# Small TensorE products moved behind the next projection at each phase opening, and the sigmoid table loaded earlier

## The chip, the cores and the metric

The kernel runs on one core of one Trainium2 chip. Its time is the device time in microseconds (us) of one execution; three runs of the kernel before lie between 1514.94 and 1518.55 us, with a median of 1517.14 us. Five engines work side by side, each through its own instructions in order: TensorE (PE, with its weight loads shown apart as PEld), VectorE (DVE), ScalarE (ACT), GpSimd (POOL) and SyncE (SP, which starts the transfers).

## The reference

Two layers work on 256 positions of width 1024, in float32. Each layer has three sub-layers, and each sub-layer is wrapped in two norms.

```
x = x + 0.5 * rmsnorm(swiglu(rmsnorm(x, g)))      # FFN 1
h = rmsnorm(x, g);  P = h @ W_in                  # mixer: one projection,
A, B, C = ssd(P), retention(P), attention(P)      #   columns split among three branches
y = sum_m sigmoid(gate_m) * (branch_m @ W_branch_m)
x = x + rmsnorm(y @ W_out)
x = x + 0.5 * rmsnorm(swiglu(rmsnorm(x, g)))      # FFN 2
```

swiglu is (silu(a) * b) @ W_out, where a and b are the two halves of x @ W_in. The attention has 16 query heads and 2 key/value heads and a window of 128 positions.

## The kernel before

The 256 positions are two tiles of 128 rows, t = 0 and t = 1. Every large product is made of three fast float32 products: a value is split into a rounded part and a remainder (`split`, L66: ACT rounds, DVE subtracts), and `mm3` (L86) adds up high by low, high by high and low by high. These are the rows L88 and L89 on PE. A projection of one tile t by 512 columns (`gemm`, L96) takes 8 steps of K, 24 matmuls, and adds up in one PSUM buffer `acc`. The weights come by DMA into `raw` and are split into `hl` by `units` (L71).

A phase is one sub-layer, and there are six: FFN 1, mixer, FFN 2, twice. Five times one phase ends while the next opens, and that is the place of this change:

- The phase that ends runs `close` (L308). Its last projection leaves a PSUM buffer, from which `posthalf` (L192) takes a sum of squares (ACT, L196) and a product with the gain (`yg`, DVE, L197). `postnorm` (L200) makes the factor `r` on POOL (`rstd`, L138: an add at L141, a power at L143) and updates `x` of tile 1 on DVE, in two halves (L206).
- The phase that opens needs `x` transposed. `prenorm` (L169) does it with 8 PE transposes for each tile (L178), which ACT and DVE copy out as `xT` (L182, L185), and it takes the sum of squares (L150) from which POOL makes the factor `pr`. Tile 0 is made inside the last projection of the old phase. Tile 1 is made inside an early projection of the new phase: `gemm` calls `do()` at step `at`, and two `after` edges (L105 to L110) fix its 8 transposes between two steps of that projection.
- In an FFN the opening's order is chunk 0 then chunk 1 of tile 0; the transposes of tile 1 stand in chunk 1, at step 2 (L327). Between the two chunks the first result is ready for use: `swiglu` (L121) makes `sl` by a Silu on ACT (L125) and `h` on DVE (L127), and `transposed` (L153) turns `h` by two PE transposes (L161) into `hT`.
- In the mixer `kvdt(0)` (L756) makes keys, values and the step sizes of tile 0 in one projection of 272 columns, and `main("aq0", 0, ...)` (L789) the first queries, with the transposes of tile 1 at step 5. Between them `att_kv` (L357) splits the keys (`kh` on ACT L367, `kl` on DVE L368), takes the values (`vn`, L371), and turns both by small PE products (L375, L379). `att_q` (L382) does the same for queries (L394).

What the program writes is not the order in which the engines get it. A scheduler that follows a simulated time line orders the instructions of each engine, within the data's dependencies and the edges that the program adds: `add_manual_dep` (in `after`, L91) and `issue_after(ins)`. The latter adds an edge to `ins` from each instruction of its block that runs on the engine of `ins`, and leaves the other engines free.

ACT holds the function tables of one set at a time; the row ACT_TABLE_LOAD shows where another set is brought in. The mixer uses Exp and Tanh, the FFN uses Silu. There are five such loads: at the start (L871), at the Exp of `mixer_consts` (L730, twice) and at the first Silu of each FFN 2 (L125, twice).

Of the kernel before, what the change touches and what calls it, by code (L numbers as in the profile page):

```python
# [10 lines left out]
AF = mybir.ActivationFunctionType  # L11
# [29 lines left out]
class Trunk:  # L41
# [54 lines left out]
    def gemm(self, xT, t, slots, width=512, at=None, do=None):  # L96

        ps = self.acc.tile([P, 512], F32, tag="acc", name="acc")
        n = len(slots)
        ts = slice(t * P, t * P + P)  # L100
        mid = []
        for k, (wh, wl) in enumerate(slots):
            x = xT[k // 2]
            if do and k == at:
                mid = do()  # L105
                for i in mid:
                    self.after(i, m[2])
            m = self.mm3(ps[:, :width], x[:, k % 2, 0, ts], x[:, k % 2, 1, ts], wh, wl, k == 0, k == n - 1)
            for i in mid:
                self.after(m[0], i)  # L110
            mid = []
        return ps

    def gemmT(self, ps, xT, slots, c0):
# [193 lines left out]
    def close(self, order, gemm, at, gpost, scale, nxt):  # L308

        yg, ss = {}, [self.small(2, "ss") for t in range(NT)]
        for n, t in order:
            last = (n, t) == (1, 1) and nxt
            ps = gemm(n, t, at if last else None, (lambda: nxt(0)) if last else None)
            yg[t, n] = self.posthalf(n, ps, gpost, scale, ss[t])
            if n:
                self.postnorm(t, [yg[t, 0], yg[t, 1]], ss[t], 4 * EPS, nxt is None)
        self.second = (lambda: nxt(1)) if nxt else None

    def ffn(self, i, l, xT, nxt):
        nc, A = self.nc, self.A
        xT, r = xT
        w = A[f"w_ffn{i}_in"][l]
        hT, slots = [], {}
        order = [(0, 0), (1, 0), (0, 1), (1, 1)] + [(c, t) for c in range(2, NFC) for t in range(NT)]
        at, where = 2, (1, 0)  # L327
        if self.first:
            order[1:3] = [(0, 1), (1, 0)]
            at, where = 5, (0, 0)  # L330
        for c, t in order:
            if c not in slots:
                with self.tc.issue_after(self.opened.ins) if self.first and not c else ExitStack():
                    slots[c] = self.units(w, 2 * c, fine=c < 2) + self.units(w, 2 * c + 1, fine=c < 2)
                hT += self.new_T(1, "hT")
            ps = self.gemm(xT, t, slots[c], 512, at, self.second if (c, t) == where else None)
            h = self.swiglu(ps[:, 0:256], ps[:, 256:512], r[t])
            self.transposed(hT[c:c + 1], h, t)
            if (c, t) == (2, 1) and self.first:
                self.first = None  # L340
                self.tables()
        gpost = self.gain(f"ffn{i}_post_g", l)
        slots = self.ffn_out_slots(i, l)
        nxT, nx = nxt() if nxt else (None, None)
        self.close([(0, 0), (0, 1), (1, 0), (1, 1)],
                   lambda n, t, at, do: self.gemm(hT, t, slots[n * KF:n * KF + KF], 512, at, do),
                   KF - 4, gpost, 2.0, nx)
        return nxT
# [386 lines left out]
    def mix(self, l, xT, nxt):  # L735
        nc, A = self.nc, self.A
# [19 lines left out]
        def kvdt(t):  # L756
            ps = self.gemm(xT, t, skv, 272)
            nc.vector.scalar_tensor_tensor(out=dtx[:, t], in0=ps[:, 256:272], scalar=r[t], in1=self.dtb,
                                           op0=ALU.mult, op1=ALU.add)
            self.att_kv(t, ps)  # L760

        def main(key, t, slots, at=None, do=None):
            ps = self.gemm(xT, t, slots, 512, at, do)
            n = int(key[2]) if len(key) > 2 else 0
            if key[:2] == "aq":
                self.att_q(n, t, ps)
            elif key[:2] == "rv":
                if n == 0:
                    S[f"rv{t}"] = self.t4([D], name="rv")
                o = S[f"rv{t}"][:, 512 * n:512 * n + 512]  # L770
                if n:
                    nc.scalar.activation(out=o, in_=ps, func=AF.Copy, scale=r[t])
                else:
                    nc.vector.tensor_scalar(out=o, in0=ps, scalar1=r[t], scalar2=None, op0=ALU.mult)
                S[f"rv{n}{t}"] = True
            elif key[:2] == "rg":
                g = self.silu2(ps, rh[t])
                nc.vector.scalar_tensor_tensor(out=g, in0=g, scalar=r[t], in1=gret[:, 512 * n:512 * n + 512],
                                               op0=ALU.mult, op1=ALU.mult)
                S[f"rg{n}{t}"] = g  # L780
            elif key[0] == "z":
                S[f"z{key[1]}{t}"] = self.silu2(ps, rh[t])
            else:
                self.rotate(key, t, ps)
            self.pump()

        kvdt(0)
        s0 = W(0)
        main("aq0", 0, s0, 5, self.second)  # L789
        scales(1)  # L790
        kvdt(1)
        S["dt"] = dtx
        pr = self.pbank()
        for t in range(NT):
            nc.tensor.transpose(pr[:, t], r[t].to_broadcast([P, P]), self.ident)
        S["rT"] = self.sm.tile([P, T], F32, tag="rT", bufs=1, name="rT")
        self.copy(S["rT"], pr[:, 0:2].rearrange("p t n -> p (t n)"))
        main("aq0", 1, s0)
        ci = 1
        for key in ("aq1", "rq", "rk", "rv0", "xbc0", "rv1", "xbc1", "rg0", "xbc2", "rg1"):  # L800
            slots = W(ci)
            ci += 1
            if key[0] == "x":
                c = int(key[3])
                for b in range(2):
                    ps = self.acc.tile([P, 2, T], F32, tag="acc", name="xbc")
# [9 lines left out]
        for m, gens in ((2, att), (1, ret), (0, ssd)):  # L816
            if m == 1:
                for key in ("z0", "z1"):
                    slots = W(ci)
                    ci += 1  # L820
                    for t in range(NT):
                        main(key, t, slots)
            bg = self.gain("b_gate", l, m * D)
            gate = {}
            for n in range(2):
                slots = W(ci)
                ci += 1
                for t in range(NT):
                    ps = self.gemm(xT, t, slots)
                    g = gate[n, t] = self.t2([512], name="gate")  # L830
                    nc.vector.scalar_tensor_tensor(out=g, in0=ps, scalar=r[t], in1=bg[:, 512 * n:512 * n + 512],
                                                   op0=ALU.mult, op1=ALU.add)
                    nc.scalar.activation(out=g, in_=g, func=AF.Tanh, scale=0.5)
                    self.pump()
                if n == 0:
                    for gen in gens:
                        self.finish(gen)
                    if m == 2:
                        yT = S["yT2"]
                    else:  # L840
                        yT = self.new_T(4, "yT")
                        for t in range(NT):
                            self.transposed(yT, S[f"y{m}{t}"], t)
            u = [self.units(A["w_branch"][l], 4 * m + i) for i in range(4)]
            order = [(n, t) for n in range(2) for t in range(NT)] if m else [(n, t) for t in range(NT) for n in range(2)]
            for n, t in order:
                ps = self.gemm(yT, t, u[2 * n] + u[2 * n + 1])
                g = gate[n, t]
                a = acc[t][:, 512 * n:512 * n + 512]
                if m == 2:  # L850
                    nc.vector.scalar_tensor_tensor(out=a, in0=g, scalar=1.0, in1=ps, op0=ALU.add, op1=ALU.mult)
                else:
                    nc.vector.scalar_tensor_tensor(out=g, in0=g, scalar=1.0, in1=ps, op0=ALU.add, op1=ALU.mult)
                    nc.vector.tensor_tensor(out=a, in0=a, in1=g, op=ALU.add)
                if m == 0:
                    self.transposed(ysT[2 * n:2 * n + 2], a, t)
                self.pump()
        gpost = self.gain("mix_post_g", l)
        slots = sum((self.units(A["w_out"][l], u, fine=u > 1) for u in range(4)), [])
        nxT, nx = nxt() if nxt else (None, None)  # L860
        self.close([(0, 0), (1, 0), (0, 1), (1, 1)],
# [106 lines left out]
```

## Time and profile before

| what | us |
|---|---|
| median of three runs | 1517.14 |
| the profiled execution, whole | 1515.11 |
| its span, first to last instruction | 1513.3 |
| PE busy (98% of the span) | 1488.2 |
| DVE busy (66%) | 998.5 |
| ACT busy (53%) | 808.3 |
| POOL busy (3%) | 40.4 |

The profile shows one execution of 1515.11 us, 1.81 us of which lie outside the span. PE is busy for nearly all of it, so what counts is the time that PE stands idle, 25.1 us, and the clock that it is granted, 0.991 of full speed over the span. The mixers' inner stretches have no idle PE at all: from 240 to 560 us it is busy for 320.0 of 320.0 us. Ends on PE are modelled, so starts are the better guide.

### The profile page before, as it was taken

To read this page: it belongs to the slowest core of one execution; us is meant where nothing else is said; L and a number is where in the kernel's file an instruction comes from. 1 tells how busy PE (TensorE), PEld (TensorE's weight loads), DVE (VectorE), ACT (ScalarE), POOL (GpSimd) and SP (SyncE) were. 2 spreads that over 40 slices of the span, in tenths; PEclk is the share of its full clock that TensorE was granted. 3 is DMA by queue.
4 is the path that set the end of the run, shared out by engine and by line. 5 is a ranking of instruction groups with operands and counts; after the bars stand their busy time and mean duration, and the time that the engine had idled before them with its cause. 6 is when DMAs were issued, how large, how long until landed. Compare 5 with 4: busy or idle time off the path is not lost.

```text
span 1513.3 us, 19964 instructions
## 1 busy us (share of the span) xinstructions
PE 1488.2 (98%) x7277; PEld 1236.5 (82%) x7277; DVE 998.5 (66%) x1647; ACT 808.3 (53%) x1392; POOL 40.4 (3%) x80
## 2 busy tenths in 40 slices
PE   8999999999999999999999999999999999999998
PEld 6788878888888887888878888788888888778886
DVE  6654566778887676555566554767798876765643
ACT  6454465576554466444465454656665544655541
POOL 0000010000100000000000000000000000000000
PEclk9999999999999999999999999999999999999999
DMA  8654546545565555554555545564455655644551
GB/s 309 225 177 167 165 162 232 167 144 162 184 223 181 195 172 180 197 188 163 186 193 187 200 151 167 201 196 155 153 167 181 208 177 176 218 166 168 192 173 67
DMA packets 82771, 275.28 MB, mean 182 GB/s; under 512 B 11120, under 2 KB 15856, under 8 KB 82672
## 3 DMA queue, kind: packets, MB, share of 16 engines
q1 hardware_dynamic: 82384, 273.93, 53.9%
q8 instruction: 57, 0.93, 0.3%
q14 instruction: 42, 0.34, 0.1%
q10 hardware_dynamic: 288, 0.07, 0.0%
HBM read 272.86 MB, written 1.11 MB: 181 GB/s over the span
## 4 chain that ended last, share of the span: by engine, by line
PE 61%; issue 36%; DVE 1%; ACT 1%; POOL 1%; DMA 0%; SPq 0%; POOLq 0%; DVEq 0%; ACTq 0%
PE acc L88 32%; PE acc L89 16%; PE xbc L88 3%; PE xbc L89 2%; PE pT L161 1%; PE pS L420 1%; PE py L697 1%; PE po L455 1%; PE pT L178 1%; PE pb L447 1%; PE po L528 0%; DMA raw<-w_ffn_in 0%; DVE xT L185 0%; ACT xT L182 0%; ACT junk L150 0%
## 5 line engine op out<-in xcount | busy, mean ns | idle before, releaser
L88 PE MATMUL acc<-hl,xT 128*128 128x512 f32 (+1 forms) x2496 | 776.2, 393 | 3.1 <-DVE hl L69 3.0
L69 DVE TENSOR_TENSOR hl<-raw,hl 128x1024 fp32r<-128x1024 f32 (+2 forms) x544 | 592.2, 1105 | 183.0 <-ACT hl L68 164.0
L68 ACT CAST hl<-raw 128x1024 fp32r<-128x1024 f32 (+2 forms) x544 | 512.1, 956 | 255.4 <-PE acc L89 216.7
L88 PEld LDWEIGHTS acc<-hl,xT 128*128 128x128 f32 x2496 | 463.9, 189 | 95.6 <-DVE hl L69 3.2
L89 PE MATMUL acc<-hl,xT 128*128 128x512 f32 (+1 forms) x1248 | 486.7, 393 | 0.4 <-DVE xT L185 0.4
L89 PEld LDWEIGHTS acc<-hl,xT 128*128 128x128 f32 x1248 | 235.4, 189 | 49.0 <-DVE xT L185 1.4
L88 PE MATMUL acc<-hl,hT 128*128 128x512 f32 x704 | 216.9, 390 | 0.0
L88 PEld LDWEIGHTS acc<-hl,hT 128*128 128x128 f32 x704 | 131.7, 188 | 26.9
L89 PE MATMUL acc<-hl,hT 128*128 128x512 f32 x352 | 136.4, 389 | 0.0
L88 PE MATMUL acc<-hl,yT 128*128 128x512 f32 x384 | 122.1, 398 | 0.0
L127 DVE SCALAR_TENSOR_TENSOR h<-acc,pr,sl 128x256 f32<-128x256 f32 x88 | 42.2, 480 | 119.6 <-ACT sl L125 119.5
L125 ACT ACTIVATE sl<-acc,pr 128x256 f32<-128x256 f32 x88 | 41.9, 476 | 145.2 <-PE acc L89 144.8
L88 PEld LDWEIGHTS acc<-hl,yT 128*128 128x128 f32 x384 | 71.5, 188 | 16.7 <-issue 2.4
L89 PEld LDWEIGHTS acc<-hl,hT 128*128 128x128 f32 x352 | 66.1, 188 | 13.9
L89 PE MATMUL acc<-hl,yT 128*128 128x512 f32 x192 | 75.5, 393 | 0.0
L88 PE MATMUL xbc<-xT,hl 128*128 128x256 f32 x384 | 72.0, 286 | 0.0
L88 PEld LDWEIGHTS xbc<-xT,hl 128*128 128x128 f32 x384 | 60.2, 191 | 2.1 <-issue 1.5
L68 ACT CAST hT<-pT 128x256 fp32r<-128x256 f32 x88 | 32.6, 372 | 44.9 <-PE pT L161 44.8
L89 PE MATMUL xbc<-xT,hl 128*128 128x256 f32 x192 | 55.4, 289 | 0.0
L69 DVE TENSOR_TENSOR hT<-pT,hT 128x256 fp32r<-128x256 f32 x88 | 36.9, 420 | 26.9 <-ACT hT L68 26.9
L197 DVE TENSOR_TENSOR yg<-acc,gain 128x512 f32<-128x512 f32 x24 | 16.6, 690 | 46.9 <-ACT junk L196 46.9
L182 ACT ACTIVATE xT<-pT,pg 128x128 fp32r<-128x128 f32 x96 | 32.0, 364 | 21.7 <-DVE xT L185 13.9
(189 smaller groups left out, 1166.4 us busy)
## 6 DMA issues: line engine op xcount, KB each, us to landing
raw<-w_ffn_in SPq DMA_DIRECT2D x176, 512.0 KB, 4.8
raw<-w_main SPq DMA_DIRECT2D x152, 512.0 KB, 4.4
raw<-w_ffn_out SPq DMA_DIRECT2D x88, 512.0 KB, 4.7
raw<-w_branch SPq DMA_DIRECT2D x48, 512.0 KB, 4.4
raw<-w_out SPq DMA_DIRECT2D x16, 512.0 KB, 4.0
bias<-rows SPq DMA_DIRECT2D x8, 512.0 KB, 6.3
L<-acs SPq DMA_DIRECT2D x8, 512.0 KB, 6.2
gain<-b_gate SPq DMA_DIRECT2D x6, 512.0 KB, 5.1
```

The lines of the kernel that those rows point to most:

```text
L68: nc.scalar.copy(out=hi, in_=src)
L69: nc.vector.tensor_tensor(out=lo, in0=src, in1=hi.bitcast(F32), op=ALU.subtract)
L88: return (mm(ps, xh, wl, start=start, stop=False), mm(ps, xh, wh, start=False, stop=False), mm(ps, xl, wh, start=False, stop=stop))
L89: mm(ps, xl, wh, start=False, stop=stop))
L125: self.last_silu = nc.scalar.activation(out=sl, in_=a, func=AF.Silu, scale=r)
L127: nc.vector.scalar_tensor_tensor(out=h, in0=b, scalar=r, in1=sl, op0=ALU.mult, op1=ALU.mult)
L161: nc.tensor.transpose(ps[:, j], src[:, (q + j) * P:(q + j + 1) * P], self.ident)
L178: made.append(nc.tensor.transpose(ps[:, j], x[:, t, (q + j) * P:(q + j + 1) * P], self.ident))
L182: last = nc.scalar.activation(out=hi, in_=ps[:, j], func=AF.Copy, scale=g[:, k:k + 1])
L197: self.nc.vector.tensor_tensor(out=y, in0=ps, in1=g[:, 512 * i:512 * i + 512], op=ALU.mult)
L420: nc.tensor.matmul(pS[:, i, :w], qT[t][:, hb + j + i], kT[:, g, hl, ks], start=hl == 0, stop=hl == 1)
L447: nc.tensor.transpose(pp[:, j], s[:, j, b * P:b * P + P], self.ident)
```

## The change

It has two parts. First, in an FFN the transposes of `h` for chunks 0 and 1 are not written right behind the `swiglu` but kept in `held`, and written after the next projection has been, with their PE instructions bound behind the last matmul of that projection (`last_mm`). In the mixer the same is done with `att_kv` of both tiles and with `att_q` of the first 8 heads. Second, a Silu on one element stands at the end of the mixer, bound behind the last Tanh of the gates.

```
         self.last_mm = m[2]                      # end of gemm

-            self.transposed(hT[c:c + 1], h, t)   # ffn
+            if held:
+                with self.tc.issue_after(self.last_mm.ins):
+                    held.pop()()
+            if c < 2:
+                held.append(lambda c=c, h=h, t=t: self.transposed(hT[c:c + 1], h, t))
+            else:
+                self.transposed(hT[c:c + 1], h, t)

-            self.att_kv(t, ps)                   # mix, kvdt
+            if held:
+                with self.tc.issue_after(self.last_mm.ins):
+                    held.pop()()
+            held.append(lambda: self.att_kv(t, ps))
+
+        held = []

-            if key[:2] == "aq":                  # mix, main
+            if held:
+                with self.tc.issue_after(self.last_mm.ins):
+                    held.pop()()
+            if key == "aq0":
+                held.append(lambda: self.att_q(n, t, ps))
+            elif key[:2] == "aq":
                 self.att_q(n, t, ps)

-                    nc.scalar.activation(out=g, in_=g, func=AF.Tanh, scale=0.5)
+                    tanh = nc.scalar.activation(out=g, in_=g, func=AF.Tanh, scale=0.5)

         gpost = self.gain("mix_post_g", l)
+        self.after(nc.scalar.activation(out=self.small(1, "w"), in_=self.mhalf, func=AF.Silu), tanh)
```

The lines of the kernel after are numbered up to 18 higher; L178 of before is L179 there, L375 is L382, L379 is L386, L161 is L162, L833 is L850.

On PE, where the first mixer opens, the kernel before has the small products of `att_kv` (L375, L379) ahead of the 8 transposes of tile 1 (`pT<-identr,x`); the 128x272 matmuls are the projection of `kvdt`, the 128x512 ones that of the first queries:

```order
L89 MATMUL acc<-hl,xT 128x272
L375 MATMUL pb<-revr,kh 128x128
L375 MATMUL pb<-revr,kl 128x128
L375 MATMUL pb<-revr,kh 128x128
L375 MATMUL pb<-revr,kl 128x128
L379 MATMUL pb<-vn,revr 128x128
L178 MATMUL pT<-identr,x 128x128 x8
L88 MATMUL acc<-hl,xT 128x512 x2
```

The kernel after has at the same place on PE:

```order
L89 MATMUL acc<-hl,xT 128x272
L179 MATMUL pT<-identr,x 128x128 x8
L88 MATMUL acc<-hl,xT 128x512 x2
L89 MATMUL acc<-hl,xT 128x512
L88 MATMUL acc<-hl,xT 128x512 x2
L89 MATMUL acc<-hl,xT 128x512
L88 MATMUL acc<-hl,xT 128x512 x2
L89 MATMUL acc<-hl,xT 128x512
L382 MATMUL pb<-revr,kh 128x128
L382 MATMUL pb<-revr,kl 128x128
L382 MATMUL pb<-revr,kh 128x128
L382 MATMUL pb<-revr,kl 128x128
```

The key products have moved behind the transposes and the rest of the query projection (9 matmuls); the value product (L386) stands another 12 matmuls later. On PE, where FFN 2 opens, the two transposes of `h` stand before, between step 1 of chunk 1 and the transposes of tile 1:

```order
L88 MATMUL acc<-hl,xT 128x512 x2
L89 MATMUL acc<-hl,xT 128x512
L161 MATMUL pT<-identr,h 128x128 x2
L178 MATMUL pT<-identr,x 128x128 x8
L88 MATMUL acc<-hl,xT 128x512 x2
```

After, the transposes of tile 1 (L179) stand there alone on PE, 18 matmuls of chunk 1 follow them, and only then the two transposes of `h`, now L162, at the end of chunk 1:

```order
L88 MATMUL acc<-hl,xT 128x512 x2
L89 MATMUL acc<-hl,xT 128x512
L88 MATMUL acc<-hl,xT 128x512 x2
L89 MATMUL acc<-hl,xT 128x512
L162 MATMUL pT<-identr,h 128x128 x2
L88 MATMUL acc<-hl,xT 128x512 x2
```

So `h` is no longer waited for between step 1 and the transposes of tile 1. On ACT the load of the Silu's set stood at that opening, between the sum of squares of the old phase's last half (L196) and the Silu:

```order
L150 ACTIVATE junk,ss<-x 128x512 x2
L196 ACTIVATE junk,ss<-acc 128x512
L125 ACT_TABLE_LOAD
L125 ACTIVATE sl<-acc,pr 128x256
L68 CAST hT<-pT 128x2x128
L182 ACTIVATE xT<-pT,pg 128x128 x8
```

After, the load stands on ACT behind the mixer's last Tanh (L850), ahead of the first rounding of `ysT`, the mixer's sum in transposed form:

```order
L850 ACTIVATE gate<-gate 128x512
L876 ACT_TABLE_LOAD
L876 ACTIVATE w<-mhalf 128x1
L68 CAST ysT<-pT 128x2x128
L68 CAST hl<-raw 128x1024
```

There are five loads in each kernel. DVE keeps its order at the openings: `h`, then the two halves of `x`, in an FFN, and `dtx`, `kl`, the two halves of `x`, `kl`, in a mixer. Inside both mixers the scheduler has dealt the small products of attention and retention among the projections anew, up to the gate projections; the number of instructions on PE is the same.

## Rows read from the trace of the kernel before

**Rows 1.** Busy time of the engines over the span, from the page.

```profile
PE 1488.2 (98%) x7277; PEld 1236.5 (82%) x7277; DVE 998.5 (66%) x1647; ACT 808.3 (53%) x1392; POOL 40.4 (3%) x80
```

**Rows 2.** Waits of PE: waiter, waited for, us in all, times, longest.

```profile
PE pT L161 <- DVE h L127: 6.4, 3, 2.4
PE pb L375 <- ACT kh L367: 4.9, 2, 2.5
...
PE pb L375 <- DVE kl L368: 1.7, 2, 0.9
```

**Rows 3.** Time line, first mixer's opening: start, us, instruction, idle before it.

```profile
206.40 0.29 PE L89 MATMUL acc<-hl,xT 128*128 128x272 f32 x1
...
207.99 0.57 POOL L143 TENSOR_TENSOR r<-v,mhalf 128x1 f32<-128x1 f32 x1
...
208.60 1.41 DVE L206 SCALAR_TENSOR_TENSOR x<-yg,r,x 128x512 f32<-128x512 f32 x2
...
209.14 0.33 PE L375 MATMUL pb<-revr,kh 128*128 128x128 f32 x1 [2.45 <-ACT kh L367]
...
210.33 0.47 PE L375 MATMUL pb<-revr,kl 128*128 128x128 f32 x1 [0.86 <-DVE kl L368]
...
211.56 1.92 PE L178 MATMUL pT<-identr,x 128*128 128x128 f32 x8
```

**Rows 4.** Time line, opening of FFN 2 in the first layer.

```profile
572.76 0.39 PE L89 MATMUL acc<-hl,xT 128*128 128x512 f32 x1
572.91 0.56 POOL L143 TENSOR_TENSOR pr<-v,mhalf 128x1 f32<-128x1 f32 x1
572.95 0.20 ACT L196 ACTIVATION_READ_ACCUMULATOR junk<-acc 128x1 f32 x1
...
573.23 1.28 ACT L125 ACT_TABLE_LOAD   x1
...
573.84 0.56 POOL L143 TENSOR_TENSOR r<-v,mhalf 128x1 f32<-128x1 f32 x1
...
574.52 0.47 ACT L125 ACTIVATE sl<-acc,pr 128x256 f32<-128x256 f32 x1
...
575.43 1.40 DVE L206 SCALAR_TENSOR_TENSOR x<-yg,r,x 128x512 f32<-128x512 f32 x2
...
575.57 0.69 PE L161 MATMUL pT<-identr,h 128*128 128x128 f32 x2 [2.42 <-DVE h L127]
...
576.23 1.97 PE L178 MATMUL pT<-identr,x 128*128 128x128 f32 x8
```

**Rows 5.** Time line, opening of FFN 1 in the second layer.

```profile
763.94 0.39 PE L89 MATMUL acc<-hl,xT 128*128 128x512 f32 x1
764.25 0.56 POOL L143 TENSOR_TENSOR pr<-v,mhalf 128x1 f32<-128x1 f32 x1
...
765.77 1.42 DVE L206 SCALAR_TENSOR_TENSOR x<-yg,r,x 128x512 f32<-128x512 f32 x2
...
765.89 0.44 PE L161 MATMUL pT<-identr,h 128*128 128x128 f32 x2 [1.56 <-DVE h L127]
...
766.58 1.97 PE L178 MATMUL pT<-identr,x 128*128 128x128 f32 x8 [0.26 <-DVE x L206]
```

**Rows 6.** Ten us at openings: busy us by engine, PEclk, DMA share, GB/s.

```profile
206.00:216.00 10.00, 6.69 (x33) 5.89 (x32) 5.22 (x14) 4.93 (x15) 2.05 (x6) 0.83 0.19 57
...
765.00:775.00 10.00, 8.86 (x36) 7.43 (x37) 5.40 (x14) 5.11 (x15) 1.51 (x4) 0.83 0.15 53
955.00:965.00 10.00, 6.80 (x24) 5.90 (x25) 5.58 (x15) 4.92 (x15) 1.75 (x5) 0.66 0.18 56
```

**Rows 7.** Time line of ACT behind the first mixer's last Tanh.

```profile
521.81 0.63 ACT L833 ACTIVATE gate<-gate 128x512 f32<-128x512 f32 x1 [0.68 <-DVE gate L831]
531.81 0.37 ACT L68 CAST ysT<-pT 128x256 fp32r<-128x256 f32 x1 [9.37 <-PE pT L161]
```

**Rows 8.** ACT by lines: the attention's scaling, mean ns after the comma.

```profile
L441 ACT ACTIVATE s<-s,rl 128x128 f32<-128x128 f32 (+1 forms) x64 | 24.1, 446 | 1.0 <-DVE rl L439 1.0
```

More of the change, by code (lines that the diff above doesn't have):

```diff
@@ L111, in gemm @@
             mid = []
+        self.last_mm = m[2]
         return ps
@@ L324, in ffn @@
         w = A[f"w_ffn{i}_in"][l]
-        hT, slots = [], {}
+        hT, slots, held = [], {}, []
         order = [(0, 0), (1, 0), (0, 1), (1, 1)] + [(c, t) for c in range(2, NFC) for t in range(NT)]
```

## Prediction

> **What bounds the kernel now.** I read first the busy times: PE works 1488.2 us of the 1513.3 us span [rows 1], so only its 25.1 us of idle time, and pieces at a lower clock, are to be had. The table of PE's waits says where: 6.4 us in three waits for `h`, 4.9 us in two for `kh` and 1.7 us in two for `kl` [rows 2], together 13.0 us, all at phase openings. These are the waits that the change names, and a reader might take 13.0 us as the gain. The time line forbids it. Behind the small products that wait stand, on PE, the 8 transposes of tile 1 of `x`, and these have a wait of their own that the first one covers. In the first mixer PE is done at 206.69 (206.40 + 0.29), waits until 209.14 and again until 210.33, and begins the transposes at 211.56; but DVE began to write `x` only at 208.60 [rows 3]. In FFN 2 `x` is written from 575.43 and the transposes begin at 576.23 [rows 4]; in the second layer's FFN 1 from 765.77 and 766.58, with a wait for `x` of 0.26 us [rows 5]. From the start of L206 to the first transpose it takes 0.80 us, and no opening can be shorter than `x` allows.
>
> **The change part by part.** The work of PE is the same in both kernels. A product that leaves a pause is done later, where PE has no idle time, so its own duration is not gained. What counts is the pauses: how long PE is idle, and how long the clock is low.
>
> Mixer openings, two alike [rows 2]. Before, PE is idle for 2.45 and 0.86 us, 3.31 together. After, the transposes are first in line and begin 0.80 us behind L206, at 209.40. L206 itself does not move: it follows `r`, ready on POOL at 208.56 (207.99 + 0.57) [rows 3], and POOL's and DVE's orders there stay. Idle: 209.40 - 206.69 = 2.71. The second four transposes need the second half of `x`, 0.70 us later (half of 1.41); four at full clock take less, so up to 0.3 us may come on top; before, this half was long there. I take 0.1. Gain 3.31 - 2.81 = 0.5 us, 1.0 for both. The moved products' inputs are ready well ahead of their new place, and the ACT and DVE parts of `att_kv` keep theirs.
>
> FFN 2 openings, two. Here the table load goes too. The Silu could use `pr` from 573.47 (572.91 + 0.56), but starts at 574.52, behind the load of 1.28 us; `h` and then `x` wait for it in DVE's order [rows 4]. The pattern without a load is FFN 1: from the start of `pr` on POOL to the transposes 766.58 - 764.25 = 2.33 us [rows 5]. Put on FFN 2 that is 572.91 + 2.33 = 575.24 against 576.23. Next late is `r`, ready at 574.40 (573.84 + 0.56), and with 0.80 us that gives 575.20 [rows 4], so it does not bind. Idle before: 2.42, and some 0.2 between the two transposes of `h` and those of `x`; after: 575.24 - 573.15 = 2.09. Gain 0.5 us, 1.0 for both. The load alone therefore brings about 1 us of earlier start, and half of it goes to the work that no longer fills the pause.
>
> The load in its new place. ACT is idle for 9.37 us behind the last Tanh, until PE gives it the first transposes of the mixer's sum [rows 7]. A load of 1.28 us and an ACTIVATE on one element fit in that: nothing. Without that cover the first `ysT` would be up to 1.5 us later in each layer. The Trainium skill has another price: the page "ScalarE: Activation LUTs", section "What ACT_TABLE_LOAD costs", gives 1283 ns for the load and a drain of about 1380 ns with it. The trace agrees on the first figure and shows no drain: the accumulator read of L196 ends at 573.15 and the load begins at 573.23 [rows 4]. With the drain, an estimate by that page would put 2 x 1.38 = 2.8 us more on the Silu's path at the two openings; the sum here goes by the rows.
>
> FFN 1 of the second layer. No load, the same order on DVE, so the transposes still begin 2.33 us behind `pr` [rows 5]. PE was idle for 1.56 and 0.26 us and used the rest of that pause for `h`; after, it is idle from 764.33 to 766.58, 2.25 us: a loss of 0.4. The very first opening has no wait for `h` (three are counted, the two FFN 2 and this one [rows 2]): nothing.
>
> Idle time: 1.0 + 1.0 - 0.4 = 1.6 us gained. Bounds: 13.0 us if `x` did not bind at all, and minus 1 us if every opening pays the 0.3 us of the second half and the FFN pauses shrink by nothing.
>
> The clock. Over ten us around an opening the mean granted clock is 0.83, and 0.66 at the second mixer [rows 6]; the two FFN 2 openings are like the first. With levels of 2.4 and 1.2 GHz, 0.83 means 3.4 us at the lower one, 0.66 means 6.8. PE is busy in nearly all of it, so each 3.4 us cost 1.7 us: six pieces, 10.2 us. It is partly chance, since the two mixers have the same pauses and differ by a piece. After, each opening has a pause of 2.1 to 2.8 us; FFN 1, idle for only 1.8 us, had its piece too. So I keep one at each, and the second piece, which came with the longest and twice broken pause, I give a third less often: 0.6 us gained. Bounds: 10.2 us gained (no piece left), 6.8 us lost (a second one at the four other openings).
>
> Inside the mixers the order is new. PE had no idle time there, so it can only lose: 0 if the scheduler's lag suffices again, and at most one ACT scaling of 0.45 us [rows 8] for each group of attention transposes, 18 in each mixer (15 before): 36 x 0.45 = 16 us. I take 0, as before with nearly as many groups.
>
> Sum: 1.6 + 0.6 = 2.2 us. The profiled execution took 1515.11 us (1513.3 and 1.81 outside), so it would take 1512.9; the median of three, 1517.14, lies 2.0 higher, about one clock piece, and I forecast for the median: 1515 us. That is under 0.2% (3 us), which is about what a measurement of this kernel can tell from no change.
>
> **The rivals.**
>
> The starts count, not the pauses: the transposes come 2.16 us earlier in each mixer (211.56 - 209.40), 0.99 in each FFN 2, and most of that stays, since the products removed ran at the low clock and run at the full one later. That would be 2 x 2.16 + 2 x 0.99 = 6.3 us less some 1.5 for the products: 4.8, with the clock term 5.4, 1511.7 us. For it: the pieces of low clock might shorten with the pause. Against: they stood at full length whether PE filled them with transposes or with matmuls, and then lie on matmuls.
>
> The waits vanish with all they bring: 13.0 us of idle time and most clock pieces, some 8 us: 1496 us. For it speaks only the table of waits; against it the starts of L206.
>
> The clock stays up. If the one, shorter pause no longer lowers it at two of five openings, 3.4 us come on top: 1511.6. For it: two broken pauses become one. Against: FFN 1, the shortest, lost its clock too.
>
> The change does not do what it says: another set is needed again before FFN 2 and the load returns. Then 1.0 us of the sum goes: 1516. Against: five loads in both orders, the Silu's behind the last Tanh.
>
> Slower, by PE's order inside the mixers. The attention starts a projection later and its groups are packed closer, while its last products stand where they stood. PE takes its instructions in order: where a transpose of the scores comes ahead of ACT's scaling, every matmul behind it stands. At 0.45 us each [rows 8] five such waits eat the gain, and 12 in both mixers make 3 us on the wrong side; half to all of the 36 groups give 1517.1 - 2.2 + 8 to 16, about 1527 us. For it: closer packing. Against: not one such wait before, in a mixer just as dense.
>
> **How the numbers follow.** The forecast, the load that returns with it, 0.58. The starts that count 0.13, the clock that stays up 0.14, the vanished waits 0.03, slower inside the mixers 0.10; the rest, 0.02, is some smaller loss. Faster by over 0.2%: 0.13 + 0.14 + 0.03, 0.30. Slower: 0.10. Within: 0.60. The range reaches from 1510.5, just past the two middle rivals, to 1518.5, where two clock pieces fall the wrong way; it leaves out the full 13 us and the slow mixers.
>
> **What the profile will show.** Right: no PE wait for `h`, `kh` or `kl` at an opening, and in their place a wait of the transposes (L179) for `x`, five times, about 2.1 us in FFNs and 2.7 in mixers, some 11.8 in all; the Silu of FFN 2 within 0.1 us of `pr`'s end; the load in ACT's pause behind the last gate Tanh; PE's idle time down by 1 to 2 us only; 3.4 us of low clock at each opening still. Wrong: openings without a pause (then `x` was not the bound); full clock through two or more; PE idle down by 4 us or more; new PE waits at the attention's transposes or score products inside the mixers.

## The result: slower, by two waits inside each mixer

The changed kernel takes 1525.45 us (median of 4 runs, 1523.56 to 1526.34) against 1516.04 us before (4 runs): ratio 1.0061, 95% interval 1.0048 to 1.0074. That is slower by 9.4 us, where 1515.0 was forecast and 1518.5 was the upper end of the range. The profiled execution took 1525.83 us, its span 1524.0 (before: 1515.11 and 1513.3).

The openings did nearly what was said of them. This is the table of PE's waits after, which answers to [rows 2] (waiter, waited for, us in all, times, longest):

```profile
PE pT L179 <- DVE x L207: 12.5, 5, 2.8
PE acc L88 <- DVE gz L565: 4.2, 2, 2.1
PE po L462 <- DVE pT L232: 3.5, 2, 1.7
...
```

The first row is the forecast one: no wait for `h`, `kh` or `kl` is left, the transposes of `x` wait five times, 12.5 us in all (forecast 11.8). The second and third are new, twice each, once per mixer: 3.8 us a mixer that stood in no table before. The rows below these (2.8, 1.4 and 0.4 us) stand in the kernel before too.

The first mixer's opening, to be held against [rows 3] (start, us, instruction, idle before it):

```profile
206.34 0.29 PE L89 MATMUL acc<-hl,xT 128*128 128x272 f32 x1
...
207.89 0.57 POOL L144 TENSOR_TENSOR r<-v,mhalf 128x1 f32<-128x1 f32 x1
...
208.51 1.41 DVE L207 SCALAR_TENSOR_TENSOR x<-yg,r,x 128x512 f32<-128x512 f32 x2
...
209.40 1.31 PE L179 MATMUL pT<-identr,x 128*128 128x128 f32 x8 [2.77 <-DVE x L207]
```

The transposes begin at 209.40, the very time worked out, 0.89 us behind L207; before they began at 211.56. The opening of FFN 2, against [rows 4]:

```profile
579.66 0.56 POOL L144 TENSOR_TENSOR pr<-v,mhalf 128x1 f32<-128x1 f32 x1
...
580.25 0.47 ACT L126 ACTIVATE sl<-acc,pr 128x256 f32<-128x256 f32 x1 [0.36 <-POOL pr L144]
...
581.19 1.41 DVE L207 SCALAR_TENSOR_TENSOR x<-yg,r,x 128x512 f32<-128x512 f32 x2
...
582.08 1.69 PE L179 MATMUL pT<-identr,x 128*128 128x128 f32 x8 [2.38 <-DVE x L207]
```

The table load is gone from ACT's row, the Silu starts 0.03 us after `pr` ends, and from `pr` to the transposes it is 2.42 us (2.33 expected). The load now stands in ACT's pause, which is 7.87 us long behind it ([rows 7] had 9.37):

```profile
528.98 1.28 ACT L876 ACT_TABLE_LOAD   x1
530.27 0.20 ACT L876 ACTIVATE w<-mhalf 128x1 f32<-128x1 f32 x1
538.34 0.37 ACT L68 CAST ysT<-pT 128x256 fp32r<-128x256 f32 x1 [7.87 <-PE pT L162]
```

So the time was lost elsewhere. Counted over two-us windows of the whole span, PE's idle time rose from 25.1 to 31.3 us, and what the lower clock costs (1 minus the granted clock, times the window) from 13.3 to 18.5 us: 11.4 us together, for a span 10.7 us longer. By stretches it is the mixers alone: from the transposes of tile 0 that open the mixer to those that open FFN 2 the first takes 372.2 us instead of 365.6, the second 371.7 instead of 366.8; the two FFNs between them take 383.0, and 382.6 before.

Ten-us windows of after, PE alone (busy, PEclk, DMA share, GB/s): the opening, as in [rows 6], and the place of the new waits.

```profile
204.00:214.00 10.00, 7.23 (x35) 0.83 0.37 133
360.00:370.00 10.00, 6.20 (x32) 0.87 0.66 211
370.00:380.00 10.00, 9.89 (x44) 0.79 0.01 2
```

The new pauses of 3.8 us bring low clock with them: the granted clock falls short of full speed by 0.13 and 0.21 of ten us each, 3.4 us lost, nearly as much as the idle time.

What happens there is to be read from the time line of the first mixer in after, PE, DVE and ACT together:

```profile
362.05 0.60 PE L454 MATMUL pb<-identr,s 128*128 128x128 f32 x4
...
362.14 2.35 DVE L69 TENSOR_TENSOR hl<-raw,hl 128x1024 fp32r<-128x1024 f32 x2
362.25 1.05 ACT L68 CAST hl<-raw 128x1024 fp32r<-128x1024 f32 x1 [0.78 <-PE acc L89]
362.48 1.03 PE L535 MATMUL po<-rv,pm 128*128 128x256 f32 x4
363.20 0.50 ACT L442 ACTIVATE s<-s,nm 128x256 f32<-128x256 f32 x1
...
364.19 0.57 ACT L230 COPY pT<-pb 128x512 f32<-128x512 f32 x1
364.41 0.68 DVE L232 COPY pT<-pb 128x512 f32<-128x512 f32 x1
...
365.24 1.08 PE L462 MATMUL po<-pT,av 128*64 128x256 f32 x8 [1.73 <-DVE pT L232]
...
365.48 1.22 DVE L69 TENSOR_TENSOR hl<-raw,hl 128x1024 fp32r<-128x1024 f32 x1
365.65 0.67 ACT L564 ACTIVATE gz<-acc,rh 128x512 f32<-128x512 f32 x1
...
367.67 0.68 DVE L565 SCALAR_TENSOR_TENSOR gz<-gz,acc 128x512 f32<-128x512 f32 x1
...
368.40 1.22 PE L88 MATMUL acc<-hl,xT 128*128 128x512 f32 x2 [2.08 <-DVE gz L565]
```

PE has transposed the scores by 362.65. Their copies out of `pb` are short (0.57 and 0.68 us) but stand behind a cast and two Exps on ACT and behind 2.35 us of weight splitting (`hl`) on DVE. PE has only the 1.03 us of L535 to put between, then the product L462 waits 1.73 us. Behind it the next projection waits 2.08 us for an `acc` buffer, which the retention gate's L565 frees; that one is behind L564 on ACT and, on DVE, behind more `hl` work and the statistics of a norm (L543). In a kernel whose mixer has no such wait (e5_q0, below) the same place reads:

```profile
348.95 0.60 PE L454 MATMUL pb<-identr,s 128*128 128x128 f32 x4
349.27 1.23 DVE L69 TENSOR_TENSOR hl<-raw,hl 128x1024 fp32r<-128x1024 f32 x1 [1.30 <-ACT hl L68]
350.89 0.57 ACT L230 COPY pT<-pb 128x512 f32<-128x512 f32 x1
...
356.19 1.08 PE L462 MATMUL po<-pT,av 128*64 128x256 f32 x8
```

From the transposes to the product it is 6.6 us there (349.55 to 356.19), with score products (L427) and projections between; DVE splits weights (`hl`) there too, and it costs PE nothing.

### The profile page after: what moved, and what is told of

The parts are those of the page before. It is cut to its first block, busy times and chain, and to the rows that moved or that the text cites. A ratio compares the mean times of both kernels' runs of the same rounds, so it can differ in the third digit from the quotient of the medians.

```text
span 1524.0 us, 19961 instructions
## 1 busy us (share of the span) xinstructions
PE 1492.7 (98%) x7277; PEld 1238.6 (81%) x7277; DVE 998.7 (66%) x1647; ACT 807.6 (53%) x1394; POOL 36.9 (2%) x80
## 4 chain that ended last, share of the span: by engine, by line
PE 58%; issue 36%; DVE 3%; ACT 1%; POOL 1%; DMA 1%; SPq 0%; POOLq 0%; DVEq 0%; ACTq 0%
PE acc L88 30%; PE acc L89 15%; PE xbc L88 3%; PE xbc L89 2%; DVE hl L69 1%; PE pT L162 1%; PE pS L427 1%; PE py L704 1%; DMA raw<-w_ffn_in 1%; PE po L462 1%; PE pT L179 1%; DVE xT L186 1%; PE pb L454 1%; ACT junk L151 1%; ACT xT L183 0%
## 5 line engine op out<-in xcount | busy, mean ns | idle before, releaser
L88 PE MATMUL acc<-hl,xT 128*128 128x512 f32 (+1 forms) x2496 | 782.5, 396 | 7.0 <-DVE gz L565 4.2
L88 PEld LDWEIGHTS acc<-hl,xT 128*128 128x128 f32 x2496 | 466.0, 191 | 98.9 <-DVE gz L565 5.1
L88 PE MATMUL acc<-hl,hT 128*128 128x512 f32 x704 | 217.0, 390 | 0.0
L88 PEld LDWEIGHTS acc<-hl,hT 128*128 128x128 f32 x704 | 131.6, 188 | 27.1
L88 PE MATMUL acc<-hl,yT 128*128 128x512 f32 x384 | 122.4, 399 | 0.0
L88 PEld LDWEIGHTS acc<-hl,yT 128*128 128x128 f32 x384 | 71.7, 188 | 17.2 <-issue 2.9
L88 PE MATMUL xbc<-xT,hl 128*128 128x256 f32 x384 | 73.1, 287 | 0.0
L88 PEld LDWEIGHTS xbc<-xT,hl 128*128 128x128 f32 x384 | 60.8, 191 | 2.0 <-DVE pr L620 0.8
L442 ACT ACTIVATE s<-s,nm 128x128 f32<-128x128 f32 (+1 forms) x64 | 28.4, 445 | 31.5 <-DVE nm L436 31.5
```

The lines of the kernel that those rows point to most:

```text
L88: return (mm(ps, xh, wl, start=start, stop=False), mm(ps, xh, wh, start=False, stop=False), mm(ps, xl, wh, start=False, stop=stop))
L442: nc.scalar.activation(out=s[:, j], in_=s[:, j], func=AF.Exp, bias=nm[:, j:j + 1], accum_out=l[:, j:j + 1])
```

## The experiments

`pump()` stands at the end of each projection and lets the attention, the retention and the third branch (`ssd`) each write one more step; the attention's first step waits until `att_q` has left the queries `aq01` of tile 1. So the theory after the result, A, is: holding these queries sets `aq01` one projection later, `pump()` starts the attention one step later, and its copies meet the gates' work. The rivals are in the expectations. All times are medians, each ratio is against the kernel before, run on the same chip in turn; its medians lie between 1516.0 and 1516.9 us. The edits are shown shortened.

| run | what is different | us | ratio, interval |
|---|---|---|---|
| e1_ffn | no hold in the mixer | 1514.9 | 0.9989, 0.9980 to 0.9997 |
| e2b_kv0 | holds `att_kv` of tile 0 alone | 1512.4 | 0.9970, 0.9959 to 0.9982 |
| e2_kv | holds `att_kv` of both tiles | 1512.0 | 0.9969, 0.9958 to 0.9980 |
| e5_q0 | and `att_q` of tile 0 | 1512.0 | 0.9977, 0.9966 to 0.9988 |
| after | and `att_q` of tile 1 | 1525.4 | 1.0061, 1.0048 to 1.0074 |
| e7_q1 | holds `att_q` of tile 1 alone | 1528.1 | 1.0074, 1.0060 to 1.0089 |
| e3_pump | after, one more pump | 1518.5 | 1.0012, 1.0003 to 1.0021 |
| e4_skip | before, one pump less | 1520.1 | 1.0017, 1.0008 to 1.0025 |
| e6_load | e2b_kv0, load not moved | 1513.1 | 0.9982, 0.9970 to 0.9993 |
| x_before | before, `x` early | 1517.6 | 1.0011, 1.0002 to 1.0021 |
| x_ffn | e1_ffn, `x` early | 1505.5 | 0.9936, 0.9923 to 0.9948 |
| x_kv0 | e2b_kv0, `x` early | 1496.5 | 0.9873, 0.9860 to 0.9885 |
| x_after | after, `x` early | 1509.5 | 0.9968, 0.9956 to 0.9980 |

**No hold in the mixer (e1_ffn).**

```
-            if held: ... held.pop()()          # kvdt and main
-            held.append(lambda: self.att_kv(t, ps))
+            self.att_kv(t, ps)
-            if key == "aq0": held.append(...)
-            elif key[:2] == "aq":
+            if key[:2] == "aq":
```

> The changed kernel without the holds in the mixer: the projections of keys and values (L767 ff.) and of the first queries hand their small products over at once, as before; the hold in the FFNs and the new place of the Silu's table load stay. Theory A (the loss sits inside the mixers: the held query product of tile 1 sets aq01 one projection later, the attention starts one pump later, and its copies then meet the gates' work on ACT and DVE): the two waits of PE inside each mixer (3.8 us a mixer) and their low-clock piece are gone; the mixer openings have their waits for kh and kl back; time 1514 to 1517 us against about 1516 before. Theory B (the loss sits in the FFN openings or in the table load's new place): 1521 to 1526, and the mixers cost nothing. Theory C (both carry some of it): 1518 to 1521.

1514.9 us: the loss is in the mixers' holds. Both new waits are gone, those for `kh` and `kl` are back.

**One more pump (e3_pump).**

```
             self.pump()                        # main's last line
+            if key == "aq1" and t == 0:
+                self.pump()
```

> The changed kernel, all its holds kept, with one more call of pump() behind the query projection aq1 of tile 0, so that the attention starts about where it did before and every later step of it has its old place. Theory A (late start of the attention): the waits for pT and gz inside the mixers are gone, PE's pauses left are those of the openings (12.5 us for x), time 1513 to 1517 us. Theory B (the holds themselves, or the load, cost it): 1522 to 1526 as the changed kernel. Theory C (any new packing of PE's order loses some): the two waits get other names but stay, 1518 to 1523.

1518.5 us: it gives back 7 of the 9.4, not all. The two waits are gone, but others came, as theory C had it, so theory A in this form is too small:

```profile
PE pT L179 <- DVE x L207: 12.3, 5, 2.8
PE xbc L88 <- DVE rb L482: 5.1, 3, 2.6
```

A fourth wait for `rb`, of 1.2 us, stands apart from these as `acc` L88. The longest of them, in the time line:

```profile
284.47 0.74 DVE L477 SCALAR_TENSOR_TENSOR ra<-acc,pr,c_rope 128x512 f32<-128x512 f32 x1
285.14 0.86 DVE L482 SCALAR_TENSOR_TENSOR rb<-acc,pr,c_rope 128x256 f32<-128x256 f32 x2
...
286.05 0.50 PE L88 MATMUL xbc<-xT,hl 128*128 128x256 f32 x2 [2.58 <-DVE rb L482]
```

A projection waits for a buffer that the retention's rope has still to read; the rope came late on DVE, behind the reductions of the scores.

**One pump less, no hold (e4_skip).**

```
-            self.pump()
+            if (key, t) != ("aq0", 1):
+                self.pump()
```

> The kernel before, with no hold at all and the load where it was; only the one pump() behind the query projection aq0 of tile 1 is left out, so that the attention starts one projection later. Theory A: this alone brings the loss: PE waits for pT (L462) and gz (L88) inside each mixer as in the changed kernel, some 3.8 us a mixer and a low-clock piece each, openings as before (13.0 us): 1525 to 1528 us. Theory B: no more than before, 1515 to 1517. Theory C: some other wait, 1518 to 1523.

1520.1 us, in theory C's range: the late start alone costs some 3 us (0.17%, interval 0.08 to 0.25), not 10. Its waits:

```profile
PE pb L447 <- ACT s L441: 2.6, 2, 1.3
...
PE acc L88 <- DVE gz L558: 0.3, 2, 0.2
```

It is the same place of the mixer (362 to 367 us), but the product waits no longer for `pT`; it is the transposes that wait, once in each mixer, for ACT's scaling, which is the form that the prediction's last rival had given, 1.3 us and not 0.45. No low clock followed these pauses in the profile.

**Which hold.** There are four holds in the mixer: `att_kv` and `att_q`, each of two tiles. e2b_kv0 keeps one, e2_kv two (its edit is the first below, e2b_kv0's both):

```
-            if key == "aq0": held.append(...)   # e2_kv, e2b_kv0
-            elif key[:2] == "aq":
+            if key[:2] == "aq":
-            held.append(lambda: self.att_kv(t, ps))   # e2b_kv0
+            if t: self.att_kv(t, ps)
+            else: held.append(lambda: self.att_kv(t, ps))
```

> The changed kernel with one hold in the mixer instead of three: only the small products of tile 0's keys and values wait until the projection of tile 1 is issued; the others go out at once. The attention then starts where it did before. Theory A: no wait inside the mixers; at their opening the products of tile 0 no longer stand ahead of the transposes of x, which wait for x alone; 1513 to 1516 us. Theory B: as the changed kernel, 1521 to 1526. Theory C: 1517 to 1521, with new waits inside the mixers.

> The changed kernel with the keys and values of both tiles held and no hold of the queries. The attention starts where it did before. Theory A (what costs is the late start of the attention together with the bunching of the query work on DVE that the hold of the queries brings, 6.1 us between the one-more-pump kernel and the one-hold kernel): no waits inside the mixers, 1511 to 1514 as with one hold. Rival (the second hold already disturbs the mixers): 1515 to 1520, with waits of the projections for rb as in the one-more-pump kernel.

1512.4 (0.6 us below theory A's range) and 1512.0 us (within it): holding keys and values is harmless, and it gains 2.5 us on e1_ffn. Then the queries, of tile 0 (e5_q0: `if (key, t) == ("aq0", 0)` holds) and of tile 1 alone (e7_q1: `("aq0", 1)` holds, `att_kv` doesn't):

> The changed kernel with both tiles of keys and values held, and of the first queries only tile 0; the products of tile 1's queries go out at once, so aq01 is set, and the attention starts, where it did before. Holding no query gave 1512.0 us, holding both and adding a pump 1518.5 (PE waits for rb, 5.1 us), holding both 1525.4. Theory A (the held products of tile 1 are what costs, by the late start and by rope work that meets that of the next queries on DVE): 1511 to 1514 us, no waits inside the mixers. Rival (any held query bunches the rope work of two tiles on DVE): 1516 to 1520, with waits of projections for rb near 280 us.

> The changed kernel with one hold in the mixer, that of tile 1's first queries, and none of keys, values or tile 0's queries; FFN holds and the moved load stay. It is the one-part-alone test: without any hold in the mixer it took 1514.9 us, with all but this one 1512.0, with all 1525.4. Theory A (this one hold carries the whole loss): PE waits for pT at L462 and for gz at L88 inside both mixers, some 3.8 us idle and one to two low-clock pieces of 1.7 us each a mixer, and the openings keep their 6.6 us for kh and kl: 1523 to 1528 us. Rival (it only costs together with the other holds, which close PE's order up): 1516 to 1520, close to the 1520 of the kernel that merely starts the attention one pump later.

1512.0 us, within theory A's range, and 1528.1, at the upper end of theory A's: of the four holds one, `att_q` of tile 1, carries all the loss. The waits of e7_q1 are those of after, beside the openings':

```profile
PE acc L88 <- DVE gz L565: 4.1, 2, 2.1
PE po L462 <- DVE pT L232: 3.5, 2, 1.7
```

**The load at its old place (e6_load).** The Silu in the mixer's closing projection is left out of e2b_kv0.

> The kernel with one hold in the mixer and those in the FFNs (1512.4 us), without the Silu in the mixer's closing projection, so the table load stands at the openings of FFN 2 again. By the prediction's step (the load brings x about 1 us earlier at these two openings, and nothing else): the transposes there wait for x some 3.1 us instead of 2.15 and 2.3, PE idle up by 1.8 us in all, 1513.5 to 1515.5. Rival (the load is hidden at the opening, or its new place costs as much as the old one): 1511.5 to 1513.

Its transposes wait 14.3 us in five waits against 12.4 with the load moved, so 1.9 us over two openings: the step of 1 us is right. The time, 1513.1 us, falls between the two ranges: 0.7 us by the medians, 1.8 by the ratios, whose intervals overlap. In the profile the two longer pauses (3.26 and 3.18 us) had full clock behind them. So the gain of the moved load is shown in idle time and not in the time.

**`x` early.** If `x` bounds the openings, it has to come sooner. In before it is late because of the order on ACT: the last projection ended at about 566 us, but its sum of squares (L196) ran at 572.46, behind eight copies of the next phase's transposes and that phase's own sum of squares (L150):

```profile
565.96 0.39 PE L89 MATMUL acc<-hl,ysT 128*128 128x512 f32 x1
...
570.70 0.37 ACT L182 ACTIVATE xT<-pT,pg 128x128 fp32r<-128x128 f32 x1 [0.42 <-DVE xT L185]
...
572.46 0.60 ACT L196 ACTIVATE junk<-acc 128x512 bf16<-128x512 f32 x1
```

The edit lets only four copies go ahead:

```
+    def prenorm(self, xT, t, g, r, defer=False):
+        out(range(CUT))                          # CUT = 4: copies 0..3
+        if defer: self.rest = rest               # copies 4..7, sum of squares, rstd
+        else: rest()
     # close: behind posthalf and postnorm of the last half
+            if last:
+                self.rest()
```

> The kernel before with that edit alone (four copies ahead of the closing sums, the rest behind). There the small products that wait for h, kh and kl stand ahead of the transposes in PE's order. Theory X, as the prediction worked it out (x bounds the opening, the products only fill its pause): with x early the next late thing are the small products, whose waits remain nearly whole: PE idle down by 0 to 3 us, 1512 to 1517. Rival Y (late copies cost): 1517 to 1525. Rival V (the pauses all hang on x, even those of the products): 1498 to 1505.

> The kernel with the holds in the FFNs and the moved table load alone, and the same edit. Theory X: the FFN openings lose their pauses for x (6.8 us in three) and some of their low-clock pieces, the mixer openings keep the waits for kh and kl (6.6 us): 1503 to 1509 us. Rival Y: 1512 to 1520. Rival V: as with the hold in the mixer, 1495 to 1503.

> The kernel with the one hold in the mixer (keys and values of tile 0), the hold in the FFNs and the moved table load, and one more edit: in the last projection of a phase only the first four copies of the next phase's transposes stand ahead of the closing sums; the other copies, the sum of squares and its root follow them. So ACT reaches the sum of squares of the old phase's last half some us sooner and x, for which all five openings wait 12.4 us in all, is written sooner. Theory X (x bounds every opening, the small products no longer do): the waits of the transposes for x shrink to a quarter or vanish, and with them most of the low-clock pieces (1.7 us each): 1495 to 1503 us, against 1512.4 without the edit. Rival Y (what was put behind takes the place: the copies and the sum of squares of the new phase come late, and the first projections or their scaling by r wait instead): 1510 to 1520, with new waits at the openings. Rival Z (each opening keeps its low-clock piece whatever the pause): 1502 to 1506.

> The whole change (all holds, the moved load) with the earlier x of the fast kernel: four copies ahead of the closing sums, the rest behind. Theory A: the openings and the mixers are separate; the openings gain the 16 us that the same edit gained with one hold (1512.4 to 1496.5), the mixers keep their waits for pT and gz with two low-clock pieces each: 1508 to 1511 us. Rival (the mixers' waits come from where the opening ends, so that an earlier x removes them): 1495 to 1500. Rival (they grow, since ACT and DVE have the late copies besides): 1512 to 1520.

Theory X holds for x_kv0 and x_ffn within its numbers, and theory A for x_after. x_before, 1517.6 us, came out 0.6 us above X's upper end and in the range of rival Y (late copies cost); its idle time rose by 3.6 us instead of falling by 0 to 3. PE's waits in x_before:

```profile
PE pT L162 <- DVE h L128: 6.4, 3, 2.4
PE acc L90 <- DVE xT L190: 5.8, 5, 1.5
PE pb L392 <- ACT kh L384: 5.5, 2, 2.7
...
PE acc L89 <- ACT xT L187: 0.8, 1, 0.8
```

and in x_kv0:

```profile
PE acc L89 <- DVE hl L70: 3.4, 1, 3.4
PE acc L90 <- DVE xT L191: 2.1, 2, 1.1
...
PE acc L89 <- ACT xT L188: 1.4, 3, 0.5
```

The waits for `h` and `kh` do not care that `x` is early, and waits for late copies of `xT`, 6.6 us, come on top: 1.5 us slower, by X's mechanism and Y's together. With the hold (x_kv0), no wait for `x` is left, and of the 6.6 us for copies 3.5 stay, in five short waits. The mixer's opening in x_kv0, where the sum of squares (L212 there) runs 3.9 us behind the transposes of tile 0 (196.75) and not 10.1 as before (196.28 and 206.35):

```profile
200.62 0.60 ACT L212 ACTIVATE junk<-acc 128x512 bf16<-128x512 f32 x1
...
202.39 0.75 DVE L222 SCALAR_TENSOR_TENSOR x<-yg,r,x 128x512 f32<-128x512 f32 x1
204.45 0.74 DVE L222 SCALAR_TENSOR_TENSOR x<-yg,r,x 128x512 f32<-128x512 f32 x1
204.59 0.63 PE L90 MATMUL acc<-hl,xT 128*128 128x272 f32 x2 [1.05 <-DVE xT L191]
...
207.31 0.92 PE L182 MATMUL pT<-identr,x 128*128 128x128 f32 x7
```

`x` is complete at 205.19, two us before PE comes to it. And the clock stays up, here in the mixer's and FFN 2's openings:

```profile
201.00:211.00 10.00, 8.95 (x52) 1.00 0.70 257
563.00:573.00 10.00, 9.54 (x46) 1.00 0.79 287
```

Over the span, idle time and low clock come to 14.7 and 4.4 us (before: 25.1 and 13.3), 19.3 us less, against 18.3 in the span. x_kv0 is 1.3% faster than before, the best of all runs. x_after keeps both waits of the mixers (4.2 and 3.8 us) and is 13.0 us slower than x_kv0; after is 13.0 slower than e2b_kv0. So openings and mixers are separate losses that add.

## Why the prediction was wrong

- **Openings, idle time.** Right: 12.5 us of waits for `x` against 11.8, and each step of it (the Silu directly behind `pr`, the load hidden, the transposes 0.8 to 0.9 us behind the writing of `x`). The idle time of the five openings fell by 1.0 us (13.5 to 12.5) where 1.6 was forecast; 0.2 of that is a misreading, since in [rows 4], the first layer, no idle time stands between the transposes of `h` and those of `x`. That `x` bounds an opening is shown, not only argued, by x_kv0: with `x` early the five pauses shrink from 12.4 to 3.5 us.
- **The sum for the openings**, 2.2 us, had the right sign and about half the size: e2_kv, e2b_kv0 and e5_q0, which have the holds and no new wait in the mixers, are 4.2 to 4.5 us below before. The clock term was too small. Of six low-clock pieces at the openings before, five are left in after and e2_kv, four in e2b_kv0 and e5_q0, so 1.7 to 3.4 us were gained where 0.6 was expected. That comes near the rival in which the clock stays up (1511.6 us), but e4_skip, without a hold, has five pieces too, so it is not shown that this is the hold's doing. Of the FFNs' share, 2.0 us in the medians (e1_ffn), its profile shows 0.5.
- **The rival that counts the starts** is refuted by e2_kv. In its first mixer the transposes of tile 1 come 2.08 us earlier (13.20 us behind those of tile 0 instead of 15.28), but the stretch to FFN 2 is only 0.50 us shorter (365.09 instead of 365.59), as much as the pause (2.79 instead of 3.31 us), at the same loss by the clock (1.70 us). So the pauses count, as the prediction had it.
- **The step that failed** is "Inside the mixers the order is new ... I take 0". It cost 11.5 us over both mixers in the profiles, their better openings included, and 13.5 in the medians against e5_q0: 3.8 us idle in each mixer, and 3.4 us of low clock in after (1.7 in e7_q1). The upper bound of 16 us held it, but the value was taken from the wrong end: that before has no such wait in a mixer "just as dense" was no evidence, since the 6.6 us of other work between transposes and product come from the order, and the order is what changed.
- **The rival that named it** (slower by PE's order inside the mixers, 1527 us, given 0.10) had the place and nearly the time, but its mechanism is not the one of after. The scaling on ACT is not waited for; the copies of the transposed scores and the release of an `acc` buffer by the gate are, both because ACT and DVE have queued work ahead of them. Its many small waits were two large ones. Its own form appears in e4_skip alone, which costs some 3 us. That 1527 us came near 1525.4 is therefore partly luck.
- **What this cost follows from.** The hold of tile 1's queries alone (e7_q1). That it is the attention's late start was my first explanation and is only part of it: starting late without the hold costs some 3 us, and undoing the late start with the hold in place leaves 6 us by another wait. Why holding these queries and starting late together make 13 us and not 3 is not settled below the level of the order: the trace shows which instruction waits for which, not why the order puts 1.0 us of work there instead of 6.6. Open too is part of e4_skip's loss: in its profile the two mixers are 3.0 us longer than before's, of which the waits make 2.9 us, a low-clock piece less in the second takes off 1.7, and for the other 1.8 neither a wait nor the clock accounts; outside the mixers it is 1.2 us longer.

## What to carry to other kernels

A wait that covers another is worth little alone: moving the small products, with the load, gained 4.5 us at best, making `x` early lost 1.5, and all together gained 19.6; so ask of each pause what is ready last, then what is ready last but one, and move both. A product that is held back holds back everything that is started by its having been issued: here holding what no start waits for (keys and values, the queries of tile 0) did no harm, and holding what sets a flag (the queries of tile 1) cost 13 us, of which the late start alone makes some 3. And where a step generator's order changes, the absence of waits before says nothing of after; what counts is how much other work stands between a producer and its reader.

## What the runs showed of the hardware

Where an opening, or a mixer of after, loses time by the lower clock, it is 1.70 to 1.72 us or twice that: pieces of 3.4 us at the lower of the two levels. Whether one follows a pause is not settled by its length here: 1.81 us of idle time in the second layer's FFN 1 had one before, 2.57 us in e3_pump (284 us) and 3.26 us in e6_load (573 us) had none. No piece followed the pauses of 0.46 to 1.05 us, five in x_kv0, nor the 1.45 us in each mixer of e4_skip. So the same order of work takes different times: 24 executions of the kernel before on one chip (in turn with e6_load) have spans from 1511.0 us at a mean granted clock of 0.993 to 1517.0 at 0.989. An edit worth less than such a difference shows in a profile's idle time, and not in the time of a single execution.
